# A 32-byte pad ahead of all tiles: shifting where tiles begin in a hybrid attention and retention layer

## The chip, the cores and the metric

The kernel runs on one core of one Trainium2 chip. The metric is the device time of one execution in microseconds (us); lower is better. The time is the median of several runs.

## What is computed

One layer of a streaming encoder, for 2048 prompt frames and 64 frames of a running stream (2112 tokens in all), model width 1024, all in fp32. The reference, cut to what matters here:

```python
a = _rmsnorm(hp, norm1[l])
qa, ka, va, qr, kr, vr, gr = _project(a, w_in[l], pos_p)
attn_o = _swa_prompt(qa, ka, va, sinks[l])          # banded attention, window 128, chunks of 64
ret_o, s_p = _retention_prompt(qr, kr, vr)          # chunkwise retention with a running state
hp = hp + _mix_out(attn_o, ret_o, gr, w_out[l])     # output projection 1024 -> 1024
hp = hp + _sqrelu_mlp(_rmsnorm(hp, norm2[l]), w_up[l], w_down[l])   # 1024 -> 4096 -> 1024
...
y_prompt = _rmsnorm(hp, norm_f)
```

The layer also returns the newest keys and values and the retention states.

## The kernel before, in words

Every matmul is made from two or three products of reduced-precision parts: a tensor x is split into a high part h (a copy rounded to the matmul type fp32r) and a low part l = x - h. The helper `split` (L519) does it with one ScalarE copy (L520) and one VectorE subtraction (L521). The products are h·h, h·l and l·h.

The work goes through four stages, one after the other on TensorE.

1. **Input projection, attention and retention** (to about 690 us). `group` (L573) multiplies a token tile (the stationary operand `xh`, `xl`) by 384 or 512 columns of the input weights (the moving operand `w`), at L586, L587 and L589. Between these groups a small planner puts the steps of attention (`att_a` to `att_e`) and retention (`ret_a` to `ret_e`), each when its inputs are due. Their tiles are in the pool `wk`. The products of attention with its values are at L366 (256 columns); the retention output is transposed at L462 and its copy `mr` goes to DRAM at L465, the attention output `mix` at L375. In this stage the order of TensorE and of the SP queue is written out by hand.
2. **Output projection** (about 693 to 887 us). `out_part` (L825) has 1,152 matmuls of 352 columns at L844 to L846: stationary `wo`, moving `mhl`.
3. **The MLP up** (about 888 to 1536 us). The MLP uses a seven-product block scheme. `up_pair` (L970) has 4,032 matmuls of 352 columns at L983 to L985: stationary `wu`, moving `ah` and `al`.
4. **The MLP down** (about 1530 to 2181 us), then the final norm. The loop at L1132 has 4,032 matmuls of 352 columns at L1149 to L1151: stationary `wd`, moving `vh` and `vl`.

**Where the tiles lie.** A tile occupies the same bytes in each of the 128 partitions, and a pool lays its tiles next to one another. Pools come from two ends: those opened plainly are laid upwards from the low end, behind a few constants of the system, and those opened with `side="right"` are laid downwards from the high end. In the program of this kernel the pools lie as follows (byte address in a partition, and what is left over at a division by 128; all tiles but a few small ones of a pool have the same remainder):

| pool | end | what it holds | first byte | remainder of 128 |
|---|---|---|---|---|
| const | low | `idf`, `idr`, `ones`, small vectors | 16,512 | 0 (`idf`, `idr`, `ones`) |
| qp | low | `w` (512 columns), `mhl`, `ah`, `al`, `vh`, `vl`: the moving operands | 18,848 | 32 |
| k1, wk | low | tables and all tiles of attention and retention | 108,960 | 64, and 0 from `ro` on (`ro`, `mr`, `mix`) |
| ar | low | `rr`, `rv`: raw data of the moving operands | 108,960 | 32 |
| xp | high | `xh`, `xl`, `xr`: the stationary operand of stage 1 | 164,768 | 32 |
| wB | high | `w` of 384 columns | 204,768 | 96 |
| op, up, xp2 | high | work tiles, `C`, `H` | from 121,312 | 96 |
| wp | high | `wo`, `wu`: the stationary operand of stages 2 and 3 | 172,000 | 96 |
| wd | high | `wd`: the stationary operand of stage 4 | 172,000 | 96 |
| wr | high | `upr`, `dr`: raw weights as they come from DRAM | 204,768 | 96 |

The high end's last byte is 229,343. The largest low pool ends at 163,968, and the lowest tile of a high pool at that time begins at 164,768.

Of the kernel before, what the change touches and what calls it, by code (L numbers as in the profile page):

```python
# [11 lines left out]
F32 = mybir.dt.float32  # L12
# [27 lines left out]
def body(ctx, tc, xt, xd, xtok, w1, wout, wup, wdn, gains, sinks, ck, cv, sret, rot, rdec, qdec, dmask,  # L40
# [4 lines left out]
    cp = ctx.enter_context(tc.tile_pool(name="const", bufs=1))  # L45
# [7 lines left out]
    uscr = dp.tile([4, 128, 16, 512], F32, name="uscr")  # L53
    sscr = dp.tile([4, 4, 128, 2048], F32, name="sscr")

    idf = cp.tile([128, 128], F32, name="idf")
    make_identity(nc, idf)
    idr = cp.tile([128, 128], F32R, name="idr")
# [1228 lines left out]
```

## Time and profile before

| | |
|---|---|
| median of 3 runs | 2193.49 us (2192.36 to 2194.59) |
| the profiled execution, first to last instruction | 2193.5 us |
| TensorE matmuls busy | 2173.8 us, 99% of the span |
| TensorE weight loads busy | 2087.9 us, 95% |
| VectorE busy | 1525.5 us, 70% |
| ScalarE busy | 1139.5 us, 52% |
| GpSimd busy | 426.2 us, 19% |
| mean granted TensorE clock | 0.996 |

In the rows of the profile PE is TensorE's matmul side and PEld its weight loads, DVE is VectorE, ACT is ScalarE and POOL is GpSimd. A row of instruction groups names the line, the engine, the operation, the tile written and the tiles read, the shape and the count; behind the bar stand the busy time in us and the mean time of one in ns, and behind the second bar the idle time just ahead of these instructions and what ended it. Matmuls overlap, so the duration of one is longer than the distance from one to the next.

### The profile page before, as it was taken

How to read it: one execution, taken by the hardware profiler on the slowest of the kernel's cores; microseconds unless marked ns; L12 is line 12 of the kernel's file. 1: busy time of each engine (PE TensorE's matmuls, PEld its weight loads, DVE VectorE, ACT ScalarE, POOL GpSimd, SP SyncE). 2: the span in 40 equal slices, each digit the busy share in tenths (PEclk: the TensorE clock that was granted, in tenths of full speed). 3: DMA queues.
4: the chain of work that ended last, by engine and by line, in shares of the span. 5: the costliest groups of instructions: out<-in, count | busy, mean ns of one | idle time of the engine just before them, and what ended most of it. 6: DMA issues, size and time to landing. Idle time of an engine off the chain costs nothing.

```text
span 2193.5 us, 35783 instructions
## 1 busy us (share of the span) xinstructions
PE 2173.8 (99%) x13170; PEld 2087.9 (95%) x13170; DVE 1525.5 (70%) x2698; ACT 1139.5 (52%) x2114; POOL 426.2 (19%) x481
## 2 busy tenths in 40 slices
PE   9999999999999999999999999999999999999998
PEld 7888897888888999999999999999999999999998
DVE  6566667666667686887787677666666876687665
ACT  6455455554445533555666566555545544554452
POOL 3544453444332312000000000000001200120011
PEclk9999999999999999999999999999999999999999
DMA  6667964698554898589799778676977777777662
GB/s 186 178 185 186 252 185 130 182 234 207 130 123 145 297 318 275 196 309 329 241 343 340 235 251 295 230 233 228 370 253 236 274 273 240 241 278 271 233 214 82
DMA packets 242927, 515.92 MB, mean 235 GB/s; under 512 B 21168, under 2 KB 128368, under 8 KB 238656
## 3 DMA queue, kind: packets, MB, share of 16 engines
q1 hardware_dynamic: 232224, 469.35, 62.9%
q0 software_dynamic: 8512, 43.29, 9.4%
q8 instruction: 103, 1.69, 0.3%
q10 hardware_dynamic: 2016, 1.00, 0.2%
q14 instruction: 72, 0.59, 0.1%
HBM read 411.19 MB, written 169.54 MB: 265 GB/s over the span
## 4 chain that ended last, share of the span: by engine, by line
PE 93%; DMA 2%; DVE 2%; ACT 1%; issue 1%; POOL 0%; SPq 0%; DVEq 0%; ACTq 0%; POOLq 0%
PE y L1151 10%; PE y L1150 10%; PE y L1149 9%; PE z L586 7%; PE z L587 6%; PE z L589 6%; PE b L984 4%; PE b L985 4%; PE b L983 4%; PE y L844 3%; PE y L846 3%; PE y L845 3%; PE c L985 3%; PE a L985 3%; PE a L984 3%; PE c L984 3%
## 5 line engine op out<-in xcount | busy, mean ns | idle before, releaser
L1151 PE MATMUL y<-vh,wd 128*128 128x352 f32 x1344 | 434.0, 323 | 0.8 <-DVE wd L521 0.8
L1150 PE MATMUL y<-vl,wd 128*128 128x352 f32 x1344 | 433.5, 323 | 0.0
L1149 PE MATMUL y<-vh,wd 128*128 128x352 f32 x1344 | 431.4, 321 | 0.0
L586 PE MATMUL z<-w,xh 128*128 128x512 f32 (+1 forms) x816 | 321.4, 394 | 1.5 <-DVE rot L210 1.5
L587 PE MATMUL z<-w,xh 128*128 128x512 f32 (+1 forms) x816 | 307.2, 377 | 1.0 <-DVE w L86 1.0
L1101 POOL TENSOR_TENSOR acc<-acc,sq 128x352 f32<-128x352 f32 x41 | 71.6, 1747 | 1212.9 <-ACT sq L1100 1212.9
L520 ACT ACTIVATE wd<-dr 128x1024 fp32r<-128x1024 f32 x168 | 177.4, 1057 | 245.4 <-PE y L1151 166.9
L520 ACT ACTIVATE wu<-upr 128x512 fp32r<-128x512 f32 x336 | 209.2, 627 | 174.8 <-PE b L985 85.5
L589 PE MATMUL z<-w,xl 128*128 128x512 f32 (+1 forms) x768 | 288.2, 375 | 0.1
L521 DVE TENSOR_TENSOR wu<-upr,wu 128x512 fp32r<-128x512 f32 x336 | 230.5, 692 | 73.5 <-ACT wu L520 57.8
L521 DVE TENSOR_TENSOR wd<-dr,wd 128x1024 fp32r<-128x1024 f32 x168 | 209.0, 1245 | 95.6 <-ACT wd L520 92.7
L1151 PEld LDWEIGHTS y<-vh,wd 128*128 128x128 f32 x1344 | 252.6, 188 | 1.1 <-DVE wd L521 1.1
L1150 PEld LDWEIGHTS y<-vl,wd 128*128 128x128 f32 x1344 | 252.5, 188 | 0.0
L1149 PEld LDWEIGHTS y<-vh,wd 128*128 128x128 f32 x1344 | 252.3, 188 | 0.0
L984 PE MATMUL b<-al,wu 128*128 128x352 f32 x576 | 185.8, 323 | 0.0
L985 PE MATMUL b<-ah,wu 128*128 128x352 f32 x576 | 185.5, 323 | 0.0
L983 PE MATMUL b<-ah,wu 128*128 128x352 f32 x576 | 184.9, 321 | 0.0
L587 PEld LDWEIGHTS z<-w,xh 128*128 128x128 f32 x816 | 155.3, 190 | 20.6 <-DVE w L86 4.2
L586 PEld LDWEIGHTS z<-w,xh 128*128 128x128 f32 x816 | 155.3, 190 | 18.6 <-ACT xh L151 1.8
L521 DVE TENSOR_TENSOR vl<-rv,vh 128x1408 fp32r<-128x1408 f32 x84 | 137.6, 1639 | 44.6 <-ACT vh L520 44.1
L589 PEld LDWEIGHTS z<-w,xl 128*128 128x128 f32 x768 | 145.0, 189 | 22.0 <-DVE xl L152 0.4
L520 ACT ACTIVATE vh<-rv 128x1408 fp32r<-128x1408 f32 x84 | 116.1, 1382 | 63.4 <-DMA rv<-vscr 40.1
(291 smaller groups left out, 4770.1 us busy)
## 6 DMA issues: line engine op xcount, KB each, us to landing
rv<-vscr SPq DMA_DIRECT2D x84, 704.0 KB, 5.5
vscr<-C SPq DMA_DIRECT2D x48, 1056.0 KB, 5.9
upr<-uscr SPq DMA_DIRECT2D x192, 256.0 KB, 4.9
dr<-sscr SPq DMA_DIRECT2D x96, 512.0 KB, 4.9
upr<-in_wup SPq DMA_DIRECT2D x144, 256.0 KB, 4.0
dr<-in_wdn SPq DMA_DIRECT2D x72, 512.0 KB, 5.6
uscr<-in_wup POOLq DMA_DIRECT2D x16, 1024.0 KB, 10.4
sscr<-in_wdn POOLq DMA_DIRECT2D x16, 1024.0 KB, 8.7
```

Of the source, the lines that this page charges most:

```text
L520: nc.scalar.activation(h, x, AF.Copy)
L521: return nc.vector.tensor_sub(l, x, h.bitcast(F32))
L586: nc.tensor.matmul(z[:, :n], xh[:, k], wh, start=k == 0, stop=False)
L587: nc.tensor.matmul(z[:, :n], xh[:, k], wl, start=False, stop=k == NK - 1 and xl is None)
L589: nc.tensor.matmul(z[:, :n], xl[:, k], wh, start=False, stop=k == NK - 1)
L983: nc.tensor.matmul(o, wh, ah[:, k], start=k == 0 and i in (1, 6, 5), stop=False, skip_group_check=True)
L984: nc.tensor.matmul(o, wh, al[:, k], start=False, stop=False, skip_group_check=True)
L985: nc.tensor.matmul(o, wl, ah[:, k], start=False, stop=k == 3 and i in (2, 4, 3), skip_group_check=True)
L1101: nc.gpsimd.tensor_add(self.acc, self.acc, sq)
L1149: nc.tensor.matmul(o, wh, vh, start=f == 0, stop=False)
L1150: nc.tensor.matmul(o, wh, vl, start=False, stop=False)
L1151: nc.tensor.matmul(o, wl, vh, start=False, stop=f == 15)
```

## The change

One tile of 8 fp32 values a partition, 32 bytes, is allocated first in the pool const. No instruction writes or reads it. It is described as a pad ahead of all tiles that makes the weights of the MLP and the output products begin at multiples of 128 bytes. No other line is touched.

```diff
--- before.py
+++ after.py
@@ -53,6 +53,7 @@
     uscr = dp.tile([4, 128, 16, 512], F32, name="uscr")
     sscr = dp.tile([4, 4, 128, 2048], F32, name="sscr")
 
+    cp.tile([128, 8], F32, name="pad")
     idf = cp.tile([128, 128], F32, name="idf")
     make_identity(nc, idf)
     idr = cp.tile([128, 128], F32R, name="idr")
```

## The prediction

> **What bounds the kernel now.** I read the page first, then the groups of instructions by line with shapes kept apart, then who made TensorE wait, then windows of the stages.
>
> ```profile
> span 2193.5 us, 35783 instructions
> PE 2173.8 (99%) x13170; PEld 2087.9 (95%) x13170; DVE 1525.5 (70%) x2698; ACT 1139.5 (52%) x2114; POOL 426.2 (19%) x481
> ```
>
> TensorE is busy for 2173.8 of 2193.5 us, so 19.7 us are all that any other engine or any transfer can have cost. The span is also the median of the runs (2193.49), so sums against the span hold for the median as they stand. What TensorE does with its time:
>
> ```profile
> L1151 PE MATMUL y<-vh,wd 128*128 128x352 f32 x1344 | 434.0, 323 | 0.8 <-DVE wd L521 0.8
> L1150 PE MATMUL y<-vl,wd 128*128 128x352 f32 x1344 | 433.5, 323 | 0.0
> L1149 PE MATMUL y<-vh,wd 128*128 128x352 f32 x1344 | 431.4, 321 | 0.0
> L985 PE MATMUL b<-ah,wu 128*128 128x352 f32 x576 | 185.5, 323 | 0.0
> L983 PE MATMUL b<-ah,wu 128*128 128x352 f32 x576 | 184.9, 321 | 0.0
> L846 PE MATMUL y<-mhl,wo 128*128 128x352 f32 x384 | 123.6, 322 | 0.0
> ```
>
> The idle time ahead of each of these groups is zero or 0.8 us: stages 2 to 4 never wait for an operand. The pace is read from the timeline, since the durations overlap:
>
> ```profile
> 1699.71 0.32 PE L1149 MATMUL y<-vh,wd 128*128 128x352 f32 x1
> ...
> 1700.18 0.32 PE L1149 MATMUL y<-vh,wd 128*128 128x352 f32 x1
> ...
> 1700.67 0.32 PE L1149 MATMUL y<-vh,wd 128*128 128x352 f32 x1
> ```
>
> Six matmuls (two triples) take 0.96 us, so one begins every 0.160 us, while one is shown as 0.323 us: two are always in flight, and a duration is about twice a distance. The 1,152 + 4,032 + 4,032 = 9,216 matmuls of stages 2 to 4 make 1474.6 us at this pace, two thirds of the span. So the change can matter in two ways only: by the pace of matmuls, or by the 19.7 us in which TensorE stands. Those lie here (columns: length, then busy time and count of PE, PEld, DVE, ACT, POOL, granted clock, DMA share, GB/s):
>
> ```profile
> 0.00:12.00 12.00, 10.16 (x38) 8.57 (x39) 6.71 (x14) 7.92 (x14) 0.71 (x7) 1.00 0.85 261
> 12.00:110.00 98.00, 95.52 (x502) 80.07 (x501) 60.93 (x154) 51.95 (x146) 49.04 (x70) 0.98 0.59 173
> 110.00:300.00 190.00, 188.19 (x1098) 166.61 (x1098) 126.82 (x361) 102.12 (x334) 92.03 (x134) 1.00 0.77 211
> 300.00:400.00 100.00, 95.94 (x529) 83.98 (x528) 71.17 (x183) 56.51 (x164) 42.56 (x55) 0.98 0.45 131
> 1527.00:2180.00 653.00, 652.16 (x4076) 651.87 (x4075) 446.53 (x468) 318.47 (x323) 71.61 (x41) 1.00 0.72 250
> 2180.00:2193.50 13.50, 4.82 (x28) 4.09 (x26) 5.28 (x15) 1.27 (x4) 1.60 (x3) 0.64 0.40 107
> ```
>
> Start and end hold 1.8 + 8.7 us, stage 1 from 12 to 400 us holds 2.5 + 1.8 + 4.1 = 8.4 us, the down stage 0.8.
>
> **What the change moves.** The pad issues nothing: no instruction, transfer or wait is added or removed, and none has another size. It takes 32 bytes at the low end. By the table of pools, everything laid upwards from there begins 32 bytes later: the moving operands of the big stages (`w` of 512 columns, `mhl`, `ah`, `al`, `vh`, `vl`) go from remainder 32 to 64 of 128, `rv` and `rr` likewise, the tiles of `wk` from 64 to 96 and from 0 to 32. The pools of the weights hang from the high end. That end is fixed and has remainder 96, so `wo`, `wu`, `wd` and their raw tiles stay at 96 unless the layout is not as I read it. On this reading the described aim is not met; the weights do not move, and the operand that streams past them does. The gap of 800 bytes between low and high pools takes the 32, and which tiles of later pools overlie which earlier ones stays the same, so no wait on a reused tile changes.
>
> **Price of the moving operand, 32 to 64.** The trace has matmuls whose moving operand lies at each remainder concerned:
>
> ```profile
> L589 PE MATMUL z<-w,xl 128*128 128x512 f32 x512 | 201.5, 394 | 0.0
> L589 PE MATMUL z<-w,xl 128*128 128x384 f32 x256 | 86.7, 339 | 0.1
> L366 PE MATMUL po<-pl,hl 128*128 128x256 f32 x64 | 18.0, 281 | 0.0
> L366 PE MATMUL po<-pm,vd 128*128 128x256 f32 x64 | 18.0, 281 | 0.0
> ```
>
> `w` of 512 columns lies at 32, `w` of 384 at 96, `pl` and `pm` at 64. From 384 to 512 columns a duration grows by 55 ns, 0.43 ns a column. Carried back to 256 columns that is 339 - 128 x 0.43 = 284; the rows at remainder 64 show 281. The same line gives 339 - 32 x 0.43 = 325 for 352 columns, where the rows at remainder 32 show 321 to 323, 2 to 4 below it as well. So the deviation of 3 ns is there at both remainders, and I take zero for the move. The ends: a gain of 3 ns of duration if the 281 is owed to the remainder, and a loss of 2 ns, the difference between L1149 and its two neighbours, if that lead hangs on where `vh` lies. Both are priced under the rivals.
>
> [...]
>
> **Price of the weights, had they moved.** Weight loads at several remainders:
>
> ```profile
> L1149 PEld LDWEIGHTS y<-vh,wd 128*128 128x128 f32 x1344 | 252.3, 188 | 0.0
> L587 PEld LDWEIGHTS z<-w,xh 128*128 128x128 f32 x816 | 155.3, 190 | 20.6 <-DVE w L86 4.2
> L462 PEld LDWEIGHTS prt<-idf,ro 128*128 128x128 f32 x64 | 8.9, 139 | 3.5
> L402 PEld LDWEIGHTS ptr<-idf,qk 128*128 128x128 f32 x128 | 15.9, 140 | 4.7 <-POOL qk L211 1.2
> ```
>
> `wd` at 96 loads in 188 ns and `xh` at 32 in 190. The transposes load quicker, but among them `ro`, a multiple of 128, takes 139 and `qk` at 64 takes 140. A multiple of 128 is worth at most 1 ns of a load that already runs beside the matmul ahead of it. Price: zero.
>
> **ScalarE, VectorE, GpSimd.** The copies and subtractions at the two remainders:
>
> ```profile
> L520 ACT ACTIVATE vh<-rv 128x1408 fp32r<-128x1408 f32 x84 | 116.1, 1382 | 63.4 <-DMA rv<-vscr 40.1
> L1001 ACT ACTIVATE C<-C 128x1408 f32<-128x1408 f32 x48 | 66.1, 1378 | 4.1 <-DVE C L998 4.1
> L1002 ACT ACTIVATE C<-C 128x1408 f32<-128x1408 f32 x48 | 65.6, 1366 | 0.1
> ```
>
> The same 1,408 elements take 1382 ns at remainder 32 and 1366 to 1378 at 96, 1.2% apart at most. In stages 2 to 4 TensorE's busy time covers whatever changes. If that cover were gone, 1.2% of the 116.1 us of `vh` copies is 1.4 us. In stage 1 the 8.4 us of TensorE's waiting follow the chain of these engines: 1.2% of it is 0.1 us either way.
>
> **Transfers.**
>
> ```profile
> mscr<-mr POOLq DMA_DIRECT2D x32, 128.0 KB, 4.1
> mscr<-mix POOLq DMA_DIRECT2D x32, 128.0 KB, 3.3
> ```
>
> `mr` and `mix` have the same size and remainder and land 0.8 us apart, so what else is on the queues outweighs the address. In the chain of waits one `mr` transfer of stage 1 stands with 10.29 us:
>
> ```profile
> 98.83 10.29 DMA mscr<-mr
> ```
>
> I take zero, with 0.8 us either way for that one place; the loads of stages 3 and 4 are covered by TensorE.
>
> [...]
>
> **The clock.** Two rows of windows hold a granted clock below 1 in stage 1:
>
> ```profile
> 30.00:90.00 60.00, 57.98 (x309) 48.80 (x309) 34.98 (x99) 26.53 (x84) 31.06 (x44) 0.97 0.36 111
> 360.00:370.00 10.00, 9.56 (x51) 9.27 (x52) 8.91 (x24) 4.24 (x15) 4.44 (x7) 0.83 0.18 54
> ```
>
> 60 x 0.03 = 1.8 and 10 x 0.17 = 1.7 us are lost there, behind gaps of TensorE. [...]
>
> **The sum.** Pace 0, weights 0, other engines 0, transfers 0: 2193.5 us. Its own range adds the ends: 1.1 (spread of the runs) + 1.7 (clock) + 0.1 + 0.8 = 3.7 us, so 2189.8 to 2197.2. About 0.2%, 4.4 us, is what a measurement of this kernel can tell from no change.
>
> **Rivals.**
> - *The weights do move to multiples of 128*, because the high end moves with the pad or the layout is otherwise than I read it. For: the description says so. Against: the fixed high end. By the weight-load rows the time is the same, 2193.5.
> - *Moving operands at multiples of 64 stream quicker.* For: 281 against 284. Against: the 352-column rows are as far below the line at remainder 32. A duration holds two distances, so 3 ns are 1.5 ns a matmul; 9,216 and the 512-column ones of stage 1 (544 + 544 + 512 = 1,600) make 10,816 x 1.5 = 16.2 us: 2177.3.
>
> ```profile
> L586 PE MATMUL z<-w,xh 128*128 128x512 f32 x544 | 222.6, 409 | 1.5 <-DVE rot L210 1.5
> L587 PE MATMUL z<-w,xh 128*128 128x512 f32 x544 | 213.9, 393 | 1.0 <-DVE w L86 1.0
> ```
>
> - *The lead of the first matmul of a triple is lost* (slower). L1149 and L983 are 2 ns shorter than what follows them, though all three lines of a triple do the same work, so it may hang on how `vh` and `ah` lie against the weights at 96; at 64 it would go. The busy time of L1149 is 434.0 - 431.4 = 2.6 us below L1151's, so per stage about 2.6, and taken at the full 2 ns for 1,344 + 1,344 matmuls 5.4 us: 2198.9. It decides once L1149 and L983 show 323. Against: a lead that belongs to the order of the triple, not to addresses, stays.
>
> **How the numbers follow.** Forecast (the low tiles move, nothing is gained) 0.74; weights move and nothing is gained 0.08; quicker stream 0.10; lost lead 0.08. So same is 0.82, faster 0.10, slower 0.08. The range runs from the forecast's low end, 2189.8, to the near rival on the slow side, 2198.9, and leaves out one in ten.
>
> **What would show it.** The rows of L1149 to L1151 and L983 to L985 at 321 to 323, six matmuls in 0.96 us, LDWEIGHTS of `wd` at 188, TensorE busy within 2 us of 2173.8 and the same counts of instructions. Durations of the 352-column rows at 320 or less would make it wrong towards faster, L1149 at 323 towards slower; a new idle time ahead of TensorE's rows in stage 1 would show a wait that I have not seen.

## The result, and the profile after

| | before | after |
|---|---|---|
| median | 2193.65 us (4 runs) | 2216.89 us (2215.57 to 2219.03, 4 runs) |
| profiled execution, span | 2193.5 us | 2214.5 us |

The ratio is 1.0106, with a 95% interval of 1.0093 to 1.0119: the kernel is slower by 1.06%, 23.2 us. That lies outside the forecast's range.

In the compiled program the pad does what the prediction read: every low pool begins 32 bytes later and no high pool moves. `vh`, `vl`, `ah`, `al` and `mhl` lie at remainder 64 of 128, the weights `wo`, `wu` and `wd` still at 96. So the described aim, weights at multiples of 128, is not met. Instructions, their order and their waits are the same ones.

The first two lines of the page after:

```profile
span 2214.5 us, 35783 instructions
PE 2196.0 (99%) x13170; PEld 2106.9 (95%) x13170; DVE 1526.3 (69%) x2698; ACT 1138.8 (51%) x2114; POOL 425.8 (19%) x481
```

TensorE is busy for 22.2 us longer, and the time in which it stands fell from 19.7 to 18.5 us. So nothing new is waited for; the matmuls themselves are slower. The groups by line with shapes kept apart (line numbers are one higher than before):

```profile
L1150 PE MATMUL y<-vh,wd 128*128 128x352 f32 x1344 | 438.9, 327 | 0.0
L1152 PE MATMUL y<-vh,wd 128*128 128x352 f32 x1344 | 436.8, 325 | 0.5 <-DVE wd L522 0.5
L1151 PE MATMUL y<-vl,wd 128*128 128x352 f32 x1344 | 433.3, 322 | 0.0
L587 PE MATMUL z<-w,xh 128*128 128x512 f32 x544 | 224.3, 412 | 1.5 <-DVE rot L211 1.5
L588 PE MATMUL z<-w,xh 128*128 128x512 f32 x544 | 215.8, 397 | 0.2 <-DVE w L87 0.2
L984 PE MATMUL b<-ah,wu 128*128 128x352 f32 x576 | 187.6, 326 | 0.0
L590 PE MATMUL z<-w,xl 128*128 128x512 f32 x512 | 203.0, 396 | 0.0
```

The first product of an MLP triple went from 321 to 327 or 326 ns (L1149 and L983 before), the third from 323 to 325, the second stayed within 1 ns. In stage 1 the 512-column rows went from 409, 393 and 394 to 412, 397 and 396. The weight loads and the copies of the down stage on the page after:

```profile
L1150 PEld LDWEIGHTS y<-vh,wd 128*128 128x128 f32 x1344 | 254.9, 190 | 0.0
L1152 PEld LDWEIGHTS y<-vh,wd 128*128 128x128 f32 x1344 | 252.1, 188 | 0.8 <-DVE wd L522 0.8
L521 ACT ACTIVATE vh<-rv 128x1408 fp32r<-128x1408 f32 x84 | 115.9, 1380 | 61.8 <-DMA rv<-vscr 42.0
```

A load takes 188 to 190 ns where 188 was shown, a copy 1380 where 1382 was. The pace shows best in a long window of TensorE's rows alone, in the up stage and the down stage (columns: length, PE busy and count, granted clock, DMA share, GB/s). Before:

```profile
900.00:1500.00 600.00, 600.00 (x3751) 1.00 0.81 278
1560.00:2160.00 600.00, 600.00 (x3752) 1.00 0.73 254
```

After:

```profile
900.00:1500.00 600.00, 600.00 (x3696) 1.00 0.80 273
1560.00:2160.00 600.00, 599.47 (x3696) 1.00 0.74 256
```

At the same full clock and without idle time, 600 us hold 3,696 matmuls in place of 3,751. One begins every 600 / 3696 = 162.3 ns in place of 160.0, 1.5% more. The output projection, up and down stages have 9,216 such matmuls.

By the starts of TensorE's instructions, stage 1 takes 694.8 us (692.8 before), the output projection 195.8 (194.6), up 658.3 (648.9), down 653.5 (644.9), the end 12.1 (12.4). The differences are +2.0, +1.2, +9.4, +8.6 and -0.3, together the 21.0 us by which the spans differ. For stage 1 the +2.0 is too little, as the granted clock differs there. The prediction's two windows of a lower clock read as follows after the change:

```profile
30.00:90.00 60.00, 58.46 (x310) 49.24 (x311) 33.63 (x95) 26.64 (x86) 30.49 (x43) 0.97 0.33 106
360.00:370.00 10.00, 8.42 (x53) 8.02 (x54) 9.84 (x25) 5.26 (x18) 4.19 (x7) 1.00 0.30 92
```

The first loss is there as before. The second, 0.83 over 10 us or 1.7 us, fell in the profile of before and not in that of after. So 1.7 us of what stage 1 lost by the change are hidden.

### The profile page after: what moved, and what is told of

The parts are those of the page before. It is cut to its first block, busy times and chain, and to the rows that moved or that the text cites. A ratio compares the mean times of both kernels' runs of the same rounds, so it can differ in the third digit from the quotient of the medians.

```text
span 2214.5 us, 35783 instructions
## 1 busy us (share of the span) xinstructions
PE 2196.0 (99%) x13170; PEld 2106.9 (95%) x13170; DVE 1526.3 (69%) x2698; ACT 1138.8 (51%) x2114; POOL 425.8 (19%) x481
## 4 chain that ended last, share of the span: by engine, by line
PE 91%; DMA 3%; DVE 3%; ACT 1%; issue 1%; POOL 0%; SPq 0%; DVEq 0%; ACTq 0%; POOLq 0%
PE y L1150 10%; PE y L1152 10%; PE y L1151 10%; PE z L587 6%; PE z L588 6%; PE z L590 6%; PE b L984 4%; PE b L986 4%; PE b L985 4%; PE y L845 3%; PE y L846 3%; PE y L847 3%; PE a L984 3%; PE a L986 3%; PE c L984 3%; PE a L985 3%
## 5 line engine op out<-in xcount | busy, mean ns | idle before, releaser
L1150 PE MATMUL y<-vh,wd 128*128 128x352 f32 x1344 | 438.9, 327 | 0.0
L1152 PE MATMUL y<-vh,wd 128*128 128x352 f32 x1344 | 436.8, 325 | 0.5 <-DVE wd L522 0.5
L1151 PE MATMUL y<-vl,wd 128*128 128x352 f32 x1344 | 433.3, 322 | 0.0
L1151 PEld LDWEIGHTS y<-vl,wd 128*128 128x128 f32 x1344 | 253.6, 189 | 0.0
L521 ACT ACTIVATE vh<-rv 128x1408 fp32r<-128x1408 f32 x84 | 115.9, 1380 | 61.8 <-DMA rv<-vscr 42.0
```

Of the source, the lines that this page charges most:

```text
L521: nc.scalar.activation(h, x, AF.Copy)
L1150: nc.tensor.matmul(o, wh, vh, start=f == 0, stop=False)
L1151: nc.tensor.matmul(o, wh, vl, start=False, stop=False)
L1152: nc.tensor.matmul(o, wl, vh, start=False, stop=f == 15)
```

## The experiments

Three theories could explain a slower stream without a new wait:

- **Theory 1, distance.** What counts is where the streamed operand lies against the weights of its matmuls, not where either lies by itself. The pad moved one and not the other, from 64 bytes apart to 32 (modulo 128).
- **Theory 2, own remainder.** A streamed operand at remainder 64 is slower than one at 32.
- **Theory 3, other traffic.** The shift makes TensorE's reads meet those of other engines or of transfers.

Below, a layout is written [streamed, weights], the remainders of 128 in the MLP: before is [32, 96], after [64, 96]. Times are medians, with the ratio to the kernel before run on the same chip. The time of a triple (three products) is three times the mean difference between the starts of consecutive matmuls in the trace, with the gaps of waiting left out: 480.2 (up) and 480.0 ns (down) before, 487.2 and 486.6 after. In stage 1 it hangs by about 0.5 ns on where a gap begins.

### TensorE alone, 16 pairings

Products of 352 columns with nothing beside them but one ScalarE copy every 48 matmuls, streamed and stationary operands at A = 0, B = 32, C = 64, D = 96 of 128 in all pairings. The layer itself is left out.

```python
for X in "ABCD":                    # streamed: mhX, mlX
    for Y in "ABCD":                # weights:  whY, wlY
        mm(y, whY, mhX); mm(y, whY, mlX); mm(y, wlY, mhX)
```

> The layer is left out: TensorE alone runs the down stage's triples (three matmuls of 352 columns on 128x128 weights) on copies of one input and one weight tile that begin 0 (A), 32 (B), 64 (C) or 96 (D) bytes behind a multiple of 128: all sixteen pairs of moving operand (mh, ml) and weights (wh, wl), 384 matmuls each, no other engine writing beside them but one copy every 48 matmuls. Theory 1 (distance: the weights that load beside a running matmul and the operand it streams disturb each other when they lie 32 of 64 bytes apart, as 96 and 64 do, and not at 0 of 64, as 96 and 32 do): A with A and C, B with B and D, C with A and C, D with B and D show about 322 ns a matmul, the other eight about 325. Theory 2 (the moving operand's own place): all four rows with C are about 325, those with B 322, whatever the weights. Theory 3 (traffic of the other engines and transfers meets TensorE's reads): all sixteen alike within 1 ns.

The whole took 1040.67 us. Rows of equal addresses (two) and of addresses 64 apart, from the groups by line:

```profile
L76 PE MATMUL y<-mhB,wlB 128*128 128x352 f32 x128 | 41.7, 326 | 0.0
L76 PE MATMUL y<-mhC,wlC 128*128 128x352 f32 x128 | 41.7, 326 | 0.0
...
L76 PE MATMUL y<-mhB,wlD 128*128 128x352 f32 x128 | 41.4, 324 | 0.0
```

Triples take 481.1 to 481.3 ns at 64 apart (A with C, B with D and the reverse), 483.5 to 485.1 at 32 apart, 486.4 to 488.4 at equal remainders. Pairs of the same distance agree wherever they lie, and pairs with the same streamed operand don't. So Theory 2 falls for this kernel, and Theory 3 cannot be all of it, as nothing else runs but those copies. But equal remainders are worst here, which the kernels below contradict; the high and low parts of this kernel lay 128 bytes apart modulo 256, which the second grid below mends.

### The aim itself: weights at multiples of 128

A pad of 96 bytes at the high end alone: [32, 0].

```diff
+    ctx.enter_context(tc.tile_pool(name="padr", bufs=1, side="right")).tile([128, 24], F32, name="padr")
     wB = early.enter_context(tc.tile_pool(name="wB", bufs=8, side="right"))
```

> Pad of 96 bytes at the high end instead, none at the low end: weights go from remainder 96 to 0, moving operands stay at 32. Theory 1: distance 32 of 64, slow as after, 2210 to 2220 us. Theory 2: moving operand as before, 2191 to 2196. Theory 3: the low tiles are as before, 2191 to 2198.

2200.01 us, ratio 1.0029 [1.0017, 1.0041]. Theory 1 expected a slower MLP at 32 apart, and that misses: triples take 480.0 ns, as the down rows show.

```profile
L1152 PE MATMUL y<-vh,wd 128*128 128x352 f32 x1344 | 433.4, 322 | 0.0
L1150 PE MATMUL y<-vh,wd 128*128 128x352 f32 x1344 | 433.4, 322 | 0.0
L587 PE MATMUL z<-w,xh 128*128 128x512 f32 x544 | 225.0, 414 | 1.9 <-DVE rot L211 1.5 <-ACT w L85 0.4
L588 PE MATMUL z<-w,xh 128*128 128x512 f32 x544 | 216.5, 398 | 1.0 <-DVE w L86 1.0
```

The loss is in stage 1, where the pad moved `xh` against `w`: 414 and 398 in place of 409 and 393. Weights at multiples of 128 bring nothing. Here the weights lie 32 below the streamed operand modulo 128, after the change 32 above; the sign must count.

### Both pads: the change, and 96 bytes at the high end

[64, 0], the streamed operand exactly where the change puts it. The diff is the change's line and the line above.

> The change's pad of 32 at the low end and 96 at the high end: moving operands at 64, weights at 0. Theory 1: distance 0 of 64 again, 2191 to 2197 us. Theory 2: 2213 to 2220, as after. Theory 3: the low tiles are as after, 2213 to 2220.

2197.58 us, ratio 1.0015 [1.0006, 1.0024]. The up and down windows:

```profile
900.00:1500.00 600.00, 600.00 (x3751) 1.00 0.81 277
1560.00:2160.00 600.00, 600.00 (x3752) 1.00 0.74 256
```

That is the pace of before with `vh` and `ah` at 64. Theory 2 falls in the whole kernel. The time is 0.6 us above the end that Theory 1 gave, and what is left over before lies in stage 1 (512-column triples 697.3 to 697.5 ns, against 687.2 before).

### Only the streamed operands of the big stages move

32 bytes ahead of `qp`, and 96 behind it, so that all other tiles keep their remainder.

```diff
+    ctx.enter_context(tc.tile_pool(name="padq", bufs=1)).tile([128, 8], F32, name="padq")
     qp = ctx.enter_context(tc.tile_pool(name="qp", bufs=8))
...
+    ctx.enter_context(tc.tile_pool(name="padk", bufs=1)).tile([128, 24], F32, name="padk")
     k1 = late.enter_context(tc.tile_pool(name="k1", bufs=1))
```

> Only the pool of the moving operands is shifted by 32 (remainder 64); const is as before and k1, wk and ar lie 128 later, at the remainders of before; weights at 96. Theories 1 and 2: the whole loss, 2213 to 2220 us. Theory 3 with the other low tiles at fault: 2191 to 2197.

2221.18 us, ratio 1.0127 [1.0112, 1.0142]: the whole loss, and 1.2 us beyond the range of Theories 1 and 2. The down triples take 489.1 ns, where they take 486.6 after the change. Its windows and the row of the first product:

```profile
900.00:1500.00 600.00, 600.00 (x3697) 1.00 0.80 273
1560.00:2160.00 600.00, 600.00 (x3682) 1.00 0.74 257
```

```profile
L1151 PE MATMUL y<-vh,wd 128*128 128x352 f32 x1344 | 438.4, 326 | 0.0
```

The tiles of attention and retention, the constants and the raw tiles keep their remainders here, so the loss needs none of them.

### The reverse: all but the streamed operands move

The change, 96 bytes ahead of `qp` and 32 behind it.

```diff
+    cp.tile([128, 8], F32, name="pad")
...
+    ctx.enter_context(tc.tile_pool(name="padq", bufs=1)).tile([128, 24], F32, name="padq")
     qp = ctx.enter_context(tc.tile_pool(name="qp", bufs=8))
...
+    ctx.enter_context(tc.tile_pool(name="padk", bufs=1)).tile([128, 8], F32, name="padk")
     k1 = late.enter_context(tc.tile_pool(name="k1", bufs=1))
```

> The complement: const, k1, wk and ar at the remainders of after (32 bytes later modulo 128), the pool of the moving operands 128 bytes later and so at 32 as before. Theories 1 and 2: as before, 2191 to 2197 us. Theory 3 with the other low tiles at fault: 2213 to 2220.

2196.36 us, ratio 1.0012 [1.0002, 1.0022]; the MLP is back at 480 ns a triple. Both runs agree: the loss goes where `qp` goes. The 2.8 us that are left (before took 2193.60 us on that chip) go with `w` lying 128 bytes elsewhere modulo 256: 697.3 ns a 512-column triple.

### TensorE alone again, parts whole multiples of 256 apart

As in the layer, high and low parts now lie whole multiples of 256 bytes apart; 352, 384 and 512 columns, more offsets. The layer is left out.

```python
mm(y, WH[:, b:b+128], H[:, a:a+352]); mm(y, WH[:, b:b+128], L[:, a:a+352]); mm(y, WL[:, b:b+128], H[:, a:a+352])
```

> The layer is left out: TensorE alone again, triples as in the kernel, with the high and low parts laid as in the kernel (a whole number of 256 bytes apart, which they were not in the first grid). One line of code for each setting: 352 columns with the slices of the moving operand 1408 bytes apart as in the kernel (weights at remainder 0 and 96, moving operand at 0, 32, 64, 96), then slices 1536 or 2048 bytes apart, so that the remainder of 256 stays, for 352, 384 and 512 columns, weights at 0, moving operand at 0 to 224 in steps of 32. Theory 1 (distance of weights and streamed operand, modulo 128 or 256): (moving 32, weights 96) about 480 ns a triple, (64, 96) 486 to 489 as in the kernel after, (32, 0) 480; of 512 columns 687 at distance 0 and 698 to 700 at 32 and 224. Theory 2 (own remainder of the moving operand): equal for both places of the weights. Theory 3 (traffic of other engines is needed): (32, 96) and (64, 96) differ by less than 2 ns a triple.

1164.0 us. Groups of the layouts [32, 96] (L100), [64, 96] (L107) and [96, 96] (L114):

```profile
L100 PE MATMUL y<-mh,wh 128*128 128x352 f32 x64 | 20.6, 321 | 0.0
L100 PE MATMUL y<-mh,wl 128*128 128x352 f32 x64 | 20.7, 323 | 0.0
L100 PE MATMUL y<-ml,wh 128*128 128x352 f32 x64 | 20.6, 323 | 0.0
...
L107 PE MATMUL y<-mh,wh 128*128 128x352 f32 x64 | 20.9, 326 | 0.0
L107 PE MATMUL y<-mh,wl 128*128 128x352 f32 x64 | 20.8, 325 | 0.0
L107 PE MATMUL y<-ml,wh 128*128 128x352 f32 x64 | 20.6, 322 | 0.0
...
L114 PE MATMUL y<-mh,wh 128*128 128x352 f32 x64 | 20.6, 323 | 0.0
L114 PE MATMUL y<-mh,wl 128*128 128x352 f32 x64 | 20.5, 320 | 0.0
L114 PE MATMUL y<-ml,wh 128*128 128x352 f32 x64 | 20.5, 320 | 0.0
```

This is the change in small: 321, 323, 323 becomes 326, 322, 325 in the order of the triple, as in the layer, with no other engine at work but for a copy every 48 matmuls. Triples take 480.0, 487.7 and 476.7 ns. Theory 3 falls: the loss is there without the layer's other traffic. With weights at 0 and the streamed operand at 0, 32, 64 and 96 the triples take 480.4, 481.6, 480.3 and 487.8 ns; the pair that is slow, [96, 0], has the same distance modulo 128 as [64, 96]. The distance isn't all of it: [0, 0] and [96, 96] have the same distances, and take 480.4 and 476.7 ns. Products of 512 columns do it too (L233 equal addresses, L240 the streamed operand 32 further):

```profile
L233 PE MATMUL y<-mh,wh 128*128 128x512 f32 x64 | 24.9, 389 | 0.0
L240 PE MATMUL y<-mh,wh 128*128 128x512 f32 x64 | 25.3, 395 | 0.0
```

Their triples take 680.0 and 700.1 ns; for equal addresses 687 had been expected, from stage 1 of the layer.

### Streamed operands 96 bytes further: [0, 96]

```diff
+    cp.tile([128, 24], F32, name="pad")
     idf = cp.tile([128, 128], F32, name="idf")
```

> Pad of 96 instead of 32: moving operands at remainder 0, weights at 96, a distance of 96; stage 1 has its weights-side operand at 32, distance 32 to the 512-column operand. Theory 1, by the rows of the pad at the high end (distance 96: 480 ns a triple; 512 columns at 32: 700): 2197 to 2204 us. Theory 2, if a multiple of 128 is the best place: 2194 or less. Theory 3: the low tiles lie otherwise than before and after; open.

2198.05 us, ratio 1.0020 [1.0011, 1.0030]. The MLP is at 480.0 and 480.8 ns a triple, and stage 1 pays: its 512-column triples take 700.3 ns, the same as with the pad of 96 at the other end, where `w` and `xh` have this distance at other addresses. Theory 1's range holds, Theory 2's (2194 or less) doesn't.

### Streamed operands 64 bytes further: [96, 96]

```diff
+    cp.tile([128, 16], F32, name="pad")
     idf = cp.tile([128, 128], F32, name="idf")
```

> Pad of 64: moving operands at 96, weights at 96, distance 0; stage 1 at a distance of 64. Theory 1, by the first grid, where distance 0 was the worst (488 against 481 ns a triple, 3,072 triples): 2210 to 2225 us. Theory 2: moving operand at 96, as the 384-column operand of stage 1 that shows nothing: 2191 to 2198.

2191.82 us, ratio 0.9991 [0.9982, 1.0000]. From the first grid Theory 1 had called equal remainders the worst case, and that misses: they are the best, as the second grid has it for 96. Theory 2's range (2191 to 2198) holds here, but [64, 0] had refuted that theory. The windows hold more matmuls than before:

```profile
900.00:1500.00 600.00, 600.00 (x3763) 1.00 0.81 278
1560.00:2160.00 600.00, 600.00 (x3758) 1.00 0.72 251
```

A triple takes 478.6 (up) and 479.1 ns (down). So the theory in its first form (equal is bad, 64 is good) is given up. What stands is its core: in the layer the pace goes with the distance of the two operands.

### Equal pads at both ends: [64, 64]

The change and a pad of the same 32 bytes at the high end ahead of `wB`. The high end is laid downwards, so its pad moves the weights from 96 down to 64, while the low one moves the streamed operands from 32 up to 64: the distance goes from 64 to 0.

```diff
+    cp.tile([128, 8], F32, name="pad")
...
+    ctx.enter_context(tc.tile_pool(name="padr", bufs=1, side="right")).tile([128, 8], F32, name="padr")
     wB = early.enter_context(tc.tile_pool(name="wB", bufs=8, side="right"))
```

> The change's pad of 32 at the low end and one of 32 at the high end: all operands of stages 2 to 4 at 64, distance 0; stage 1 at distance 192 of 256. Theory 1: as with the pad of 64 at the low end alone, 2190 to 2194 us, all of the loss gone. Theory 2: moving operand at 64 as after, 2213 to 2220.

2192.23 us, ratio 0.9990 [0.9981, 0.9999]. The change with one line more loses nothing: 24.7 us less than after, with the streamed operands at the very addresses that after gives them. It was run on another chip than after, and before took 2194.45 us there.

### The change, and 32 bytes at the high end only behind stage 1

The pad stands ahead of `wr`, so stage 1 is laid out as after and the MLP as [64, 64].

```diff
+    cp.tile([128, 8], F32, name="pad")
...
+    ctx.enter_context(tc.tile_pool(name="padr", bufs=1, side="right")).tile([128, 8], F32, name="padr")
     wr = ctx.enter_context(pool(name="wr", bufs=6, side="right"))
```

> The change, with a pad of 32 at the high end behind stage 1 only: weights of the output projection and the MLP at 64 like the moving operand, stage 1 as after. Theory 1: the loss of stages 2 to 4 is gone and 4 us more, that of stage 1 stays (2.0 us by the ends of the stages, up to 6.4 by its triples): 2191 to 2196 us. Theory 2: 2213 to 2220.

2195.99 us, ratio 1.0007 [0.9999, 1.0016]: against before on that chip (2194.45) about 1.5 us are left of the 23.2, not far from what can be told from nothing. They are a difference of two things: stages 2 to 4 are a little quicker than before (up triples 478.6 ns for 480.2), and stage 1 is slower. By its profile stage 1 takes 699.1 us, 6.3 more than before. This profile has both losses of clock that before has, 0.97 from 30 to 90 us and 0.83 from 360 to 370, so these 6.3 us are the cost of the new place in stage 1, as far as one execution of each can tell.

### Weights 64 bytes lower, behind stage 1 only: [32, 32]

The kernel before, with stage 1 untouched.

```diff
+    ctx.enter_context(tc.tile_pool(name="padr", bufs=1, side="right")).tile([128, 16], F32, name="padr")
     wr = ctx.enter_context(pool(name="wr", bufs=6, side="right"))
```

> No pad at the low end; a pad of 64 at the high end only behind stage 1, so weights of the output projection and the MLP lie at 32 like the moving operand (distance 0 and 128 of 256 by turns) and stage 1 is as before. Theory 1, by the rows of the pad of 64 (478.3 to 479.1 ns a triple for 480): 384 x 1.6 + 1,344 x 1.6 + 1,344 x 0.9 = 4.0 us less, 2188 to 2191. Theory 2 (own remainder of the moving operand): 2192 to 2196, as before.

2191.87 us, ratio 0.9987 [0.9978, 0.9996]: 2.6 us less than before on that chip (2194.45), where 4.0 was expected, and 0.9 above the range of Theory 1. Its up and down windows:

```profile
900.00:1500.00 600.00, 600.00 (x3763) 1.00 0.81 277
1560.00:2160.00 600.00, 600.00 (x3758) 1.00 0.74 249
```

This version takes 0.13% less than before, with an interval that just clears 1, and 1.1% less than after.

### Is it the matmul's own weights or the next one's?

While a matmul streams, the weights of the next are loaded: in the trace of before, a load for L1149 begins at 1700.03 us, when the matmul of L1151 ahead of it begins. Single products with the operands at 0 or 128 by turns should tell the two apart. The layer is left out.

> The layer is left out: TensorE alone, single matmuls (no triples), 352 and 512 columns. Which weights does the streamed operand collide with: those that load beside it, which are the next matmul's, or its own? Moving operand and weights begin at 0 or 128 of 256, by turns. Distances 0 for all matmuls: 160 to 161 ns a matmul of 352 columns, 226.7 of 512. Distance 128 for all: 166.7 and 233.3. Own distance 0 and next 128: 166.7 and 233.3 if the next weights matter, 160 and 226.7 if its own do. Own 128 and next 0: the reverse.

645.32 us. For 512 columns, in the order: all equal, all 128 apart, own equal and next 128 apart, own 128 apart and next equal:

```profile
L93 PE MATMUL y<-mh,wh 128*128 128x512 f32 x384 | 87.4, 389 | 0.0
L100 PE MATMUL y<-mh,wh 128*128 128x512 f32 x384 | 89.9, 395 | 0.0
L107 PE MATMUL y<-mh,wh 128*128 128x512 f32 x384 | 88.0, 390 | 0.0
L114 PE MATMUL y<-mh,wh 128*128 128x512 f32 x384 | 88.7, 392 | 0.0
```

From start to start they take 226.8, 233.3, 228.3 and 230.0 ns. The mixed cases lie between the pure ones, the first nearer to its own weights' case, the second in the middle. For 352 columns the case 128 apart took 158.4 ns where 166.7 was expected, and the mixed cases took 158.9 and 163.3. It is inconclusive: which of the two loads counts stays open.

### The layouts of the layer side by side

| kernel | [streamed, weights] | weights minus streamed, mod 128 | matmuls in 1560 to 2160 us | median us |
|---|---|---|---|---|
| after | [64, 96] | 32 | 3696 | 2216.89 |
| only `qp` moves | [64, 96] | 32 | 3682 | 2221.18 |
| before | [32, 96] | 64 | 3752 | 2193.65 |
| change, 96 at the high end | [64, 0] | 64 | 3752 | 2197.58 |
| all but `qp` moves | [32, 96] | 64 | 3752 | 2196.36 |
| 96 at the high end | [32, 0] | 96 | 3752 | 2200.01 |
| 96 at the low end | [0, 96] | 96 | 3746 | 2198.05 |
| 64 at the low end | [96, 96] | 0 | 3758 | 2191.82 |
| change, 32 at the high end | [64, 64] | 0 | 3758 | 2192.23 |
| change, 32 at the high end, late | [64, 64] | 0 | 3752 | 2195.99 |
| 64 at the high end, late | [32, 32] | 0 | 3758 | 2191.87 |

The same distance gives the same pace within 14 matmuls at the different addresses of the table; among the layers only 32 is slow. The rest of the differences in the medians goes with stage 1, whose 512-column triples take 687.2 ns in before and 697 to 700 in the kernels of 2196 to 2200 us. They too go by the distance, here modulo 256: with the addresses of the compiled programs (weights minus streamed) they take about 687 ns at 0, 689 at 192, 697 at 128, and 699 to 701 at 160 and 224. Each distance occurs in two kernels or more, which agree within about 1 ns; at 128, 160 and 192 these have different addresses.

## Why the prediction was wrong, point by point

**The layout** was right: the low tiles move, the weights do not, and the aim isn't met. The rival in which the weights move fell, and its time with it: the kernel that does move them to multiples of 128 takes 2200.01 us.

**The bound** was right: the stream of matmuls holds the time, and a change could act only on its pace or on 19.7 us of standing. It acted on the pace.

**The step that failed** is the price of the moving operand: "So the deviation of 3 ns is there at both remainders, and I take zero for the move." It compared rows by the remainder of the streamed operand alone. The 512-column rows have `w` at 32, but their weights `xh` are at 32 too, a distance of 0; `pl` and `pm` at 64 stream against `hl` and `vd` at 64, again 0. The 384-column rows (`w` at 96, `xh` at 32) and the 352-column rows (32 and 96) have a distance of 64. So the rows covered the distances 0 and 64 modulo 128, at which the MLP's triples take 478.6 to 480.2 ns in the runs, and none stood at the new distance of 32, at which they take 6.6 to 7.0 ns more in after than before. That is 2.2 to 2.3 ns a matmul in place of the zero. The lesson in method: the neighbour rows must agree with the new case in everything but one thing, and the streamed operand was never looked at together with its weights.

**The lost lead** (2198.9, chance 0.08) was the rival that came true, with its place, its sign and its condition: it "may hang on how `vh` and `ah` lie against the weights at 96; at 64 it would go". Its rows show it, L1149 and L983 going above 323. Its size failed: the bound was 2 ns on the first product, the difference to its neighbours, and the first product lost 6 ns, the third 2. A lead of before bounds what can be lost only if the neighbours are the slow end, and they were not.

By triples the cost works out so. Up 1,344 x 7.0 ns = 9.4 us, down 1,344 x 6.6 = 8.9, output projection 384 x (483.2 - 479.8) = 1.3, stage 1 512 x (699.7 - 687.2) = 6.4: together 26.0 us, against 23.2 measured. The first three agree with the lengths of the stages (+9.4, +8.6, +1.2). Of stage 1's 6.4 us the profile of after shows 2.0, and 1.7 more are hidden by the loss of clock that it does not have; the kernel that has after's stage 1 and both losses shows 6.3. The remaining 2.7 us stay open.

**The quicker stream** (2177.3) fell, and a step of it was wrong as well: "a duration holds two distances, so 3 ns are 1.5 ns a matmul". The triple's durations grew by 974 - 967 = 7 ns and its starts by 487 - 480 = 7 ns: what a matmul loses is in its duration once, not twice. The second grid shows the same: mean durations of 322.2, 334.1 and 389.1 ns for 352, 384 and 512 columns go with distances of 160.0, 173.3 and 226.7, so a duration is a distance and some 161 to 162 ns, and only at 352 columns does this look like twice.

**Weight loads, the other engines, transfers**: all at zero, and nothing in the profiles speaks against it: 188 to 190 ns for a load, 1380 for a copy, TensorE's standing 18.5 for 19.7 us. What `mr`'s transfer costs can't be told beside the rest.

**The clock** has 1.7 us in the forecast's range, what the loss from 360 to 370 us takes. The profile of after lacks this loss, with a granted clock of 1.00 where before shows 0.83. TensorE's idle time just ahead is nearly the same, 2.74 us for 2.72; on what such a loss depends, no run shows.

## What to carry to other kernels

Where weights and streamed operands are laid from two ends of the memory, a pad at one end changes the distance between them, and with it the pace of the matmuls can change (here from one every 160.0 ns at 64 modulo 128 to one every 162.3 at 32). Pads at both ends push the operands towards each other, so equal pads change the distance by twice their size (here from 64 to 0); it stays the same modulo 128 where the two pads add up to 128, as 32 and 96 did. When TensorE is never idle and one layout step makes it slower with the same instructions, count matmuls in a window of full clock, and look at the two addresses together, modulo 256, not at either's alignment. Equal remainders were the best layout of the MLP here, by 0.1% against before: worth trying by one unused tile, and worth measuring, since the pattern differs with the number of columns and the sequence: in the second grid, with the streamed operand 32 bytes further than equal addresses, the rows show 322 to 323 ns for 352 columns, where equal addresses show 322 to 325, and 395 for 512 columns, where equal addresses show 389; at a constant distance of 128 modulo 256 a matmul of 352 columns begins every 166.6 ns in triples and every 158.4 in single products.

## What the runs showed of the hardware

- **A matmul with a new weight load each time costs its columns and a fixed part**: 160.0, 173.3 and 226.7 ns from start to start for 352, 384 and 512 columns in the second grid. That is 0.417 ns a column and 13.3 ns beside. Some sequences are a little quicker: 158.9 ns at [96, 96] for 352 columns.
- **On top come up to 7.6 ns a matmul by the places of the two operands**: 700.1 to 702.7 against 680.0 ns a triple of 512 columns, and 499.9 against 480.1 for 352 columns at a constant distance of 128 modulo 256 (L149 below, in the second grid). The 20 ns are 6.7 ns a matmul, the time of 16 columns.

```profile
L149 PE MATMUL y<-mh,wh 128*128 128x352 f32 x64 | 21.0, 327 | 0.0
```

- **The pattern depends on more than the distance of one matmul.** In the layer the slices of `vh` begin 1,408 bytes apart, 128 by turns modulo 256. After the change the down triples take 493.4 ns where the weights lie 32 above the slice modulo 256, and 479.9 where they lie 160 above. In the grid with a constant distance it is 160 and 128 that are slow (486.7 and 499.9), and 32 isn't (480.0). Single products at the same constant distance of 128, with no low parts between, take 158.4 ns each, or 475.2 for three. In most groups of the second grid the means of stretches of 48 matmuls repeat within 1 ns a triple, but at [64, 96] four such stretches take 485.9, 486.8, 488.3 and 489.8. A rule for a single matmul was not found.
- **Open**: what in the chip makes it so. No run shows it. The one that set a matmul's own weights against the next one's was inconclusive: its mixed cases, 228.3 and 230.0 ns for 512 columns, lie between the pure ones, 226.8 and 233.3.
